# Down projection of both SwiGLU layers by chunk pairs, from seven Strassen block products

## The chip, the cores and the metric

The kernel runs on one core of one Trainium2 chip. The metric is device time in microseconds (us) of one execution. TensorE (PE) multiplies, with its weight loads shown as PEld; VectorE (DVE), ScalarE (ACT) and GpSimd (POOL) work elementwise; transfers are issued from the queues of SyncE (SP) and POOL and carried by 16 DMA engines.

## The reference

One decoder block over 256 tokens of width 2048, all in float32:

```python
x = LN(ALPHA*x + 0.5 * (silu(x@Wg1) * (x@Wu1)) @ Wd1)      # D_FF = 5632
x = LN(ALPHA*x + mixer(x))                                 # attention heads beside an RG-LRU, then w_out
x = LN(ALPHA*x + 0.5 * (silu(x@Wg2) * (x@Wu2)) @ Wd2)
x = x + sigmoid(x @ w_ple_gate) * (p @ w_ple_proj)
```

Weights come from HBM once each: `Wg`, `Wu` are 2048x5632 and `Wd` is 5632x2048. The change touches the product with `Wd1` and `Wd2`, (256x5632) @ (5632x2048).

## The kernel before

**Precision.** A float32 product is made of three fp32r products: each operand is split into `hi` (a rounding copy on ACT, L61 or L88) and `lo` (source minus hi on DVE, L62 or L94), and hi*hi, hi*lo and lo*hi are added up in one PSUM bank.

**Weights.** A list (`make_plan`) holds every weight tile of 256 rows x 512 columns ("entry", 512 KB) in the order in which PE uses them. SP loads an entry into a `raw` buffer (5 of them, L71); ACT makes `hi`, DVE makes `lo` (9 buffers each). `advance` prepares up to 7 entries beyond the one that PE holds, and loads are issued three entries beyond the one that is cast.

**SwiGLU** (`swiglu`, L405) goes over 11 chunks of 512 hidden units. A chunk takes 8 gate entries and 8 up entries (`group_a`: per entry 16 matmuls on hi, 512 columns, and on lo, 256 columns, into four banks), evacuated by ACT and DVE (L309, L310, L414, L415, L426) and split (L61, L62) into the activations of the chunk. Then come 8 down entries of the chunk before (`down`): for each of four column blocks of 512 and each of two token blocks of 128, 12 matmuls of 512 columns into a bank, which one DVE operation adds to the accumulator `acc` in SBUF (L315 the first time, L317 after). So a chunk's down projection takes 96 matmuls and 8 additions to `acc`. The last chunk's down (`down_last`) is joined with the LayerNorm that follows.

**Order.** Every engine works its queue in the order in which the program is written; nothing is reordered. A queue waits at its head: SP for a free `raw`, ACT for a loaded `raw` and a free `hi`, DVE for `hi` or for a finished bank. POOL does little: the LayerNorm residuals, a few `lo`, some small transfers.

Of the kernel before, what the change touches and what calls it, by code (L numbers as in the profile page):

```python
# [5 lines left out]
F32 = mybir.dt.float32  # L6
# [11 lines left out]
NCH = FF // 512  # L18
# [6 lines left out]
ALPHA = 2.0 ** 0.25  # L25
# [12 lines left out]
class Block:  # L38
# [105 lines left out]
    def make_plan(self):  # L144
        i = self.i
        plan = self.plan = []

        def add(w, r0, c0, n=1, **kw):
            for j in range(n):
                plan.append({"src": self.rows2(w, r0 + 256 * j, c0), "work": False, "pool": False,  # L150
                             "parts": [slice(0, 2)], "stationary": False, **kw})

        def ffn(name):
            g, u, d = (i[f"{name}_w_{v}"] for v in ("gate", "up", "down"))
            for c in range(NCH):
# [80 lines left out]
    def group_a(self, on_block, boundary=False):  # L236
        banks = [self.bank() for _ in range(4)]
        if not boundary:
            for j in range(8):
                e = self.take()  # L240
                self.tokens_a(e, j, banks, slice(0, 256), True, on_block)
                self.done(e)
                self.tick()
            return
# [85 lines left out]
    def down(self, acts, first):  # L330
        for n in range(4):
# [71 lines left out]

    def swiglu(self, boundary):
        nc = self.nc  # L405
        pend = None
        for c in range(NCH):
            gate = []

            def on_gate(b, bank):  # L410
# [7 lines left out]
            self.group_a(on_gate, boundary and c == 0)  # L418
            if c == 1 and not boundary:
                self.res_q.append(self.tables())  # L420
            ah, al = self.wide_r(), self.wide_r()

            def on_up(b, bank):
                u = self.narrow()
                self.evac_a(bank, u)
                nc.vector.scalar_tensor_tensor(u, gate[b], 0.5, u, op0=ALU.mult, op1=ALU.mult)  # L426
                self.split(ah[:, b, :], al[:, b, :], u)
# [217 lines left out]

    def mixer(self):
        nc = self.nc
        self.v = self.wide((P, 2, 512))
        self.group_b(lambda t, bank: nc.scalar.copy(self.v[:, t, :], bank), boundary=True)
        self.hs = []  # L650
# [66 lines left out]
        self.split(self.xT[:, 2 * j:2 * j + 2, 0, :], self.xT[:, 2 * j:2 * j + 2, 1, :], raw)  # L717

    def load_p(self):
        self.praw = self.narrow(), self.narrow()  # L720
        for k in range(2):
            self.nc.sync.dma_start(self.praw[k], self.i["pT"][k * P:(k + 1) * P, :])

    def split_p(self):
        self.pT, self.pp = self.wide_r(), []
        for k in range(2):
            self.split(self.pT[:, k, :], self.pT[:, 2 + k, :], self.praw[k])

    def load_acc(self, j):
        t, h = j % 2, j // 2  # L730
# [3 lines left out]
    def build(self):  # L734
        tc = self.tc
        with (
            tc.tile_pool(name="wraw", bufs=5) as self.wraw,
            tc.tile_pool(name="whi", bufs=SLOTS) as self.whi,
            tc.tile_pool(name="wlo", bufs=SLOTS) as self.wlo,
            tc.tile_pool(name="work", bufs=12) as self.work,  # L740
# [61 lines left out]
```

## Time and profile before

| | |
|---|---|
| time, median of 3 runs (lowest to highest) | 1930.77 us (1929.12 to 1932.76) |
| the profiled execution: its time, and its span | 1930.92 us, 1929.2 us |
| PE busy | 1916.6 us, 99% |
| weight loads (PEld) busy | 1654.4 us, 86% |
| DVE, ACT, POOL busy | 1290.9 us (67%), 961.8 us (50%), 151.1 us (8%) |
| bytes moved by DMA | 375.27 MB, 195 GB/s over the span |

The span is the profiled part of an execution; 1.7 us lie around it. Busy matmuls overlap in the profile (a matmul of 512 columns is shown as about 390 ns though the next starts after some 227 ns), so the pace of PE is read from starts. The first SwiGLU lies at about 5 to 720 us of the span, the second at about 1080 to 1815 us.

### The profile page before, as it was taken

The page shows a single profiled execution, that of the slowest core. Times are in us where ns is not written, and L with a number is a line of the kernel's source. Part 1 is how long each engine was busy: PE and PEld are TensorE (multiplying, and loading weights), DVE is VectorE, ACT ScalarE, POOL GpSimd, SP SyncE. Part 2 cuts the span into 40 slices and gives each one's busy share as a digit, 9 for nine tenths or more (in the row PEclk, how much of TensorE's full clock was granted, in tenths as well). Part 3 has the DMA queues.
Part 4 walks back from the last instruction along what each step waited for, and adds up shares of the span by engine and source line. Part 5 has one row for each costly group of instructions (what it writes and reads, how often), then busy time and mean ns, then how long its engine had stood idle before and what let it go on. Part 6 is the DMA issues. An engine that isn't in the chain of part 4 may idle for free.

```text
span 1929.2 us, 26578 instructions
## 1 busy us (share of the span) xinstructions
PE 1916.6 (99%) x10244; PEld 1654.4 (86%) x10244; DVE 1290.9 (67%) x1679; ACT 961.8 (50%) x1330; POOL 151.1 (8%) x93
## 2 busy tenths in 40 slices
PE   8999999999999999999999999999999999999999
PEld 7888888888888888888888898888888888888787
DVE  6667565756665666878777786566656756565875
ACT  6544444544444446656754545444444444454552
POOL 0000000000000012301100250000000000000151
PEclk9999999999999999999999999999999999999999
DMA  9666565556655666755465466656565556655564
GB/s 318 210 214 200 172 218 196 178 175 219 208 179 178 197 207 189 226 174 164 148 193 198 148 209 221 203 175 219 171 219 177 196 173 222 195 176 176 177 220 141
DMA packets 195007, 375.27 MB, mean 195 GB/s; under 512 B 11953, under 2 KB 14657, under 8 KB 194881
## 3 DMA queue, kind: packets, MB, share of 16 engines
q1 hardware_dynamic: 193856, 370.42, 58.6%
q0 software_dynamic: 1024, 3.16, 0.5%
q8 instruction: 80, 1.31, 0.3%
q14 instruction: 47, 0.38, 0.1%
HBM read 371.43 MB, written 2.10 MB: 194 GB/s over the span
## 4 chain that ended last, share of the span: by engine, by line
PE 99%; DVE 1%; DMA 0%; issue 0%; ACT 0%; SPq 0%; POOL 0%; DVEq 0%
PE mm L205 98%; PE mm L382 1%; DVE w L62 0%; DMA raw<-in_ffn_w_gate_dram 0%; DVE lo L94 0%; PE mm L588 0%; DVE bst L360 0%; DVE acc L317 0%; ACT hi L88 0%; POOL rs L369 0%; DVE acc L372 0%; SPq L71 0%; PE mm L620 0%; PE mm L619 0%; SPq L713 0%
## 5 line engine op out<-in xcount | busy, mean ns | idle before, releaser
L205 PE MATMUL mm<-xT,hi 128*128 128x512 f32 (+1 forms) x3216 | 1096.0, 390 | 6.1 <-DVE xT L62 5.0
L88 ACT CAST hi<-raw 128x1024 fp32r<-128x1024 f32 (+1 forms) x676 | 692.8, 1048 | 603.6 <-PE mm L205 399.4
L94 DVE TENSOR_TENSOR lo<-raw,hi 128x1024 fp32r<-128x1024 f32 (+1 forms) x676 | 837.6, 1277 | 219.0 <-ACT hi L88 218.3
L205 PE MATMUL mm<-xT,lo 128*128 128x256 f32 (+1 forms) x3216 | 887.6, 276 | 0.0
L205 PEld LDWEIGHTS mm<-xT,hi 128*128 128x128 f32 x3216 | 604.9, 188 | 130.7 <-ACT hi L88 6.3
L205 PEld LDWEIGHTS mm<-xT,lo 128*128 128x128 f32 x3216 | 606.2, 189 | 1.7 <-DVE lo L94 0.7
L205 PE MATMUL mm<-hi,w 128*128 128x512 f32 x1672 | 521.4, 390 | 0.0
L205 PEld LDWEIGHTS mm<-hi,w 128*128 128x128 f32 x1672 | 313.9, 188 | 65.4
L205 PE MATMUL mm<-lo,w 128*128 128x512 f32 x836 | 325.7, 390 | 0.6 <-DVE lo L94 0.6
L310 DVE TENSOR_TENSOR w<-mm,w 128x256 f32<-128x256 f32 x200 | 83.3, 419 | 184.3 <-ACT w L309 184.3
L205 PEld LDWEIGHTS mm<-lo,w 128*128 128x128 f32 x836 | 157.0, 188 | 32.5 <-DVE lo L94 1.0
L205 PE MATMUL mm<-hi,xT 128*128 128x512 f32 (+1 forms) x584 | 178.2, 382 | 0.0
L317 DVE TENSOR_TENSOR acc<-acc,mm 128x512 f32<-128x512 f32 x184 | 122.0, 680 | 62.3 <-PE mm L205 62.3
L94 POOL TENSOR_TENSOR w<-raw,w 128x1024 fp32r<-128x1024 f32 x9 | 26.0, 2912 | 1297.8 <-ACT w L88 669.2
L309 ACT COPY w<-mm 128x256 f32<-128x256 f32 x200 | 72.5, 366 | 107.7 <-PE mm L205 107.6
L205 PEld LDWEIGHTS mm<-hi,xT 128*128 128x128 f32 x584 | 107.7, 188 | 20.1
L205 PE MATMUL mm<-lo,xT 128*128 128x512 f32 (+1 forms) x292 | 110.4, 378 | 0.0
L61 ACT CAST w<-w 128x256 fp32r<-128x256 f32 x90 | 36.5, 406 | 92.0 <-DVE w L426 92.0
L62 DVE TENSOR_TENSOR w<-w,w 128x256 fp32r<-128x256 f32 x90 | 43.2, 480 | 41.8 <-ACT w L61 41.8
L415 DVE TENSOR_TENSOR w<-w,w 128x256 f32<-128x256 f32 x88 | 38.6, 439 | 44.3 <-ACT w L414 44.3
L205 PEld LDWEIGHTS mm<-lo,xT 128*128 128x128 f32 x292 | 55.0, 188 | 9.6
L414 ACT ACTIVATE w<-w 128x256 f32<-128x256 f32 x88 | 36.8, 418 | 48.1 <-DVE w L310 48.1
(125 smaller groups left out, 624.4 us busy)
## 6 DMA issues: line engine op xcount, KB each, us to landing
raw<-in_ffn_w_up_dram SPq DMA_DIRECT2D x176, 512.0 KB, 4.7
raw<-in_ffn_w_down_dram SPq DMA_DIRECT2D x176, 512.0 KB, 4.8
raw<-in_ffn_w_gate_dram SPq DMA_DIRECT2D x175, 512.0 KB, 4.6
raw<-in_w_in_dram SPq DMA_DIRECT2D x88, 512.0 KB, 4.5
raw<-in_w_out_dram SPq DMA_DIRECT2D x32, 512.0 KB, 4.7
raw<-in_w_ple_gate_dram SPq DMA_DIRECT2D x32, 512.0 KB, 5.0
w<-in_ln_g_dram SPq DMA_DIRECT2D x12, 256.0 KB, 8.7
w<-in_ln_b_dram SPq DMA_DIRECT2D x12, 256.0 KB, 8.0
```

What stands on the lines that cost most here:

```text
L61: self.nc.scalar.copy(hi, src)
L62: (self.nc.gpsimd if pool else self.nc.vector).tensor_tensor(lo, src, hi.bitcast(F32), op=ALU.subtract)
L88: self.nc.scalar.copy(e["hi"][:, k, :], e["raw"][:, k, :])
L94: eng.tensor_tensor(e["lo"][:, k, :], e["raw"][:, k, :], e["hi"][:, k, :].bitcast(F32), op=ALU.subtract)
L205: self.nc.tensor.matmul(out, lhsT=lhsT, rhs=rhs, start=start, stop=stop, skip_group_check=True)
L309: self.nc.scalar.copy(c, bank[:, 256:])
L310: self.nc.vector.tensor_tensor(dst, bank[:, :256], c, op=ALU.add)
L317: self.nc.vector.tensor_tensor(a, a, bank, op=ALU.add)
L382: nc.tensor.transpose(bank[:, q * P:(q + 1) * P], self.acc[:, t, kb * P:(kb + 1) * P], self.ident)
L414: nc.scalar.activation(s, g, AF.Sigmoid)
L415: nc.vector.tensor_tensor(g, g, s, op=ALU.mult)
```

## The change

Two neighbouring chunks of 512 hidden units and two column blocks of 512 of `Wd` form a 2x2 block product (the two token blocks x two chunks by two chunks x two column blocks), which is taken from seven block products (`p1` to `p7`, Winograd's form of Strassen) in place of eight. Each takes two entries and 12 matmuls of 512 columns. Chunks 0 to 9 make five pairs in each SwiGLU; chunk 10 stays with `down_last`.

- `make_forms` builds, after a pair's second up group, the seven left operands (four differences and sums, seven splits of 128 x 512).
- The right operands are single blocks of `Wd` or sums of two to four of them. The sums are made by transfers that add into `raw` (`accum_op=ALU.add`, issued from POOL): `p7` is loaded by SP and then added to (`plus`); `p5`, `p6` and `p4` are grown, each from the `raw` of the one before it in the chain `p1`, `p5`, `p6`, `p4`, once that has been cast (`grow`). Each is then cast to `hi` and `lo` as any entry.
- The 14 products of a pair (two halves of `Wd`'s columns) are run one at a time between the entries of the next two chunks: after each second gate or up entry, and in chunk 10 after each one.
- There are now 7 `raw` buffers (5 before), and 8 `hi` and 8 `lo` (9 before).

```diff
-SLOTS = 9
+SLOTS = 8
+RAWS = 7
+ORDER = ("p1", "p2", "p5", "p3", "p6", "p7", "p4")
...
+        if e.get("grows"):
+            return
         e["raw"] = self.tile(self.wraw, [P, 2, 512], F32, "raw")
         for k in e["parts"]:
             self.nc.sync.dma_start(e["raw"][:, k, :], e["src"][:, k, :])
+        if e.get("plus") is not None:
+            self.nc.gpsimd.dma_start(e["raw"], e["plus"], accum_op=ALU.add)
+
+    def grow(self, e):
+        n = e.get("next")
+        if n is not None:
+            n["raw"] = e["raw"]
+            self.nc.gpsimd.dma_start(n["raw"], n["src"], accum_op=ALU.add)
...
+        self.grow(e)
...
             for c in range(NCH):
-                add(g, 0, c * 512, 8, stationary=True)
-                add(u, 0, c * 512, 8, stationary=True)
-                if c:
-                    down(d, (c - 1) * 512)
+                step = 1 if c == NCH - 1 else 2
+                for w in (g, u):
+                    for j in range(8):
+                        add(w, 256 * j, c * 512, stationary=True)
+                        if j % step == step - 1 and todo:
+                            todo.pop(0)()
+                if c % 2:
+                    todo = blocks(d, (c - 1) * 512, 0) + blocks(d, (c - 1) * 512, 2)
...
+    def product(self):
...
+        kind, n = self.products.pop(0)
+        if kind in ("p1", "p2", "p5"):
+            self.pbank[kind] = self.bank()
+        bank = self.pbank[{"p2": "p2", "p5": "p5", "p3": "p5"}.get(kind, "p1")]
+        f = self.forms[kind]
+        es = []
+        for j in range(2):
+            e = self.take()
...
+            for k in range(2):
+                q = 2 * j + k
+                self.mm_moving_w(bank, (f[:, 0, q, :], f[:, 1, q, :]), e["hi"][:, k, :], e["lo"][:, k, :],
+                                 kind in ("p1", "p2", "p5") and q == 0, q == 3)
...
+            if (t, n + h) in self.untouched:
+                self.untouched.remove((t, n + h))
+                self.nc.vector.scalar_tensor_tensor(a, a, ALPHA, bank, op0=ALU.mult, op1=op)
+            else:
+                self.nc.vector.tensor_tensor(a, a, bank, op=op)
...
+    def make_forms(self, h0, h1):
...
+        put("p1", h0[:, :, a])
+        put("p2", h1[:, :, a])
+        nc.vector.tensor_tensor(s1, h1[:, :, b], h0[:, :, b], op=ALU.subtract)
+        put("p5", s1)
+        nc.vector.scalar_tensor_tensor(s2, s1, -1.0, h0[:, :, a], op0=ALU.mult, op1=ALU.subtract)
+        nc.vector.scalar_tensor_tensor(s4, s2, -1.0, h1[:, :, a], op0=ALU.mult, op1=ALU.subtract)
+        put("p3", s4)
+        put("p6", s2)
+        nc.vector.tensor_tensor(s3, h0[:, :, a], h0[:, :, b], op=ALU.subtract)
+        put("p7", s3)
+        put("p4", h1[:, :, b])
+        self.products = [(kind, n) for n in (0, 2) for kind in ORDER]
...
             self.group_a(on_gate, boundary and c == 0, step)
...
-            self.group_a(on_up)
-            if pend is not None:
-                self.down(pend, c == 1)
-            pend = (ah, al)
+            self.group_a(on_up, step=step)
+            if c % 2:
+                self.make_forms(before, h)
+            before = h
         self.down_last(pend)
```

Each product is added to `acc` once, and its split activations are no longer made per chunk but per pair. The queues show it at two places of the first SwiGLU.

DVE at the end of the up group of chunk 1, before (`mm` a PSUM bank, `w` a work buffer, L310 to L62 the evacuation and the split of the last block, L94 a `lo`, L315 an addition to `acc`):

```order
L310 TENSOR_TENSOR w_186_1054<-mm_813,w_187_1055 128x256
L426 SCALAR_TENSOR_TENSOR w_186_1054<-w_144_801,w_186_1054 128x256
L62 TENSOR_TENSOR w_148_809<-w_186_1054,w_147_808 128x256
L94 TENSOR_TENSOR lo_1014<-raw_945,hi_1013 128x1024
L94 TENSOR_TENSOR lo_1064<-raw_967,hi_1063 128x1024
L315 SCALAR_TENSOR_TENSOR acc<-acc,mm_1073 128x512
```

And now (L350 and L528 the same evacuation, L64 the splits of the seven left operands, L423 to L429 their sums and differences, L106 a `lo`):

```order
L350 TENSOR_TENSOR w_142_795<-mm_799,w_177_1033 128x256
L528 SCALAR_TENSOR_TENSOR w_142_795<-w_139_788,w_142_795 128x256
L64 TENSOR_TENSOR w_180_1039<-w_69_384,w_180_1039 128x512
L64 TENSOR_TENSOR w_181_1042<-w_142_795,w_181_1042 128x512
L423 TENSOR_TENSOR w_178_1037<-w_142_795,w_69_384 128x512
L64 TENSOR_TENSOR w_182_1046<-w_178_1037,w_182_1046 128x512
L425 SCALAR_TENSOR_TENSOR w_178_1037<-w_178_1037,w_69_384 128x512
L426 SCALAR_TENSOR_TENSOR w_179_1038<-w_178_1037,w_142_795 128x512
L64 TENSOR_TENSOR w_183_1051<-w_179_1038,w_183_1051 128x512
L64 TENSOR_TENSOR w_184_1054<-w_178_1037,w_184_1054 128x512
L429 TENSOR_TENSOR w_179_1038<-w_69_384 128x512
L64 TENSOR_TENSOR w_185_1058<-w_179_1038,w_185_1058 128x512
```

Eleven operations of 128 x 512 (the last one follows below) now stand between the last evacuation and the next `lo`, where before the next `lo` followed at once.

POOL after its first transfers in the first SwiGLU, before (L94 are three `lo` at the first LayerNorm, at 709 us):

```order
L461 DMA posi_905<-in_pos_dram 128x2
L465 DMA w_163_904<-in_inv_dram 128x16
L94 TENSOR_TENSOR w_1217_6434<-raw_6383,w_1216_6433 128x1024
L94 TENSOR_TENSOR w_1221_6455<-raw_6389,w_1220_6454 128x1024
```

And now (L83 is a transfer that grows the `raw` of a chain, L77 the one that adds to a `p7`; `raw_800` and `raw_825` are the two halves of the chain of the first pair's first product set):

```order
L568 DMA w_157_890<-in_inv_dram 128x16
L83 DMA raw_800<-in_ffn_w_down_dram 128x2x512
L83 DMA raw_825<-in_ffn_w_down_dram 128x2x512
L83 DMA raw_800<-in_ffn_w_down_dram 128x2x512
L83 DMA raw_825<-in_ffn_w_down_dram 128x2x512
L77 DMA raw_1272<-in_ffn_w_down_dram 128x2x512
L83 DMA raw_800<-in_ffn_w_down_dram 128x2x512
L77 DMA raw_1296<-in_ffn_w_down_dram 128x2x512
L83 DMA raw_825<-in_ffn_w_down_dram 128x2x512
```

POOL's queue, which was empty here until the first LayerNorm, now carries 8 adding transfers for each half pair, and the last growth of each chain stands behind a `p7` addition that waits for SP's load.

## Rows read from the trace of the kernel before

**Rows 1.** The page: busy time by engine, and the chain that ended last.

```profile
PE 1916.6 (99%) x10244; PEld 1654.4 (86%) x10244; DVE 1290.9 (67%) x1679; ACT 961.8 (50%) x1330; POOL 151.1 (8%) x93
...
PE 99%; DVE 1%; DMA 0%; issue 0%; ACT 0%; SPq 0%; POOL 0%; DVEq 0%
```

**Rows 2.** Windows of two chunks each; length, busy (x instructions), clock, DMA, GB/s.

```profile
core 0: us, PE busy (x) PEld busy (x) DVE busy (x) ACT busy (x) POOL busy (x), PEclk, DMA share, GB/s
316.52:446.80 130.28, 130.28 (x704) 112.76 (x703) 81.59 (x104) 59.82 (x80) 0.00 (x0) 1.00 0.59 193
446.80:577.00 130.20, 130.20 (x704) 112.69 (x703) 81.59 (x104) 59.68 (x81) 0.00 (x0) 1.00 0.59 193
```

**Rows 3.** Timeline of PE: a down projection's first matmul; start, busy.

```profile
294.74 0.40 PE L205 MATMUL mm<-hi,w 128*128 128x512 f32 x1
```

**Rows 4.** Timeline of PE: the next gate group's first matmuls.

```profile
316.52 0.40 PE L205 MATMUL mm<-xT,hi 128*128 128x512 f32 x1
...
316.76 0.28 PE L205 MATMUL mm<-xT,lo 128*128 128x256 f32 x1
...
316.88 0.39 PE L205 MATMUL mm<-xT,hi 128*128 128x512 f32 x1
...
317.10 0.28 PE L205 MATMUL mm<-xT,lo 128*128 128x256 f32 x1
```

**Rows 5.** Groups on DVE, 316.5 to 447 us; busy, mean ns, idle before.

```profile
L94 DVE TENSOR_TENSOR lo<-raw,hi 128x1024 fp32r<-128x1024 f32 x48 | 56.7, 1220 | 17.4 <-ACT hi L88 17.4
L317 DVE TENSOR_TENSOR acc<-acc,mm 128x512 f32<-128x512 f32 x16 | 10.6, 681 | 6.3 <-PE mm L205 6.3
L310 DVE TENSOR_TENSOR w<-mm,w 128x256 f32<-128x256 f32 x16 | 6.7, 419 | 17.4 <-ACT w L309 17.4
L415 DVE TENSOR_TENSOR w<-w,w 128x256 f32<-128x256 f32 x8 | 3.4, 426 | 3.9 <-ACT w L414 3.9
L62 DVE TENSOR_TENSOR w<-w,w 128x256 fp32r<-128x256 f32 x8 | 3.4, 426 | 3.8 <-ACT w L61 3.8
L426 DVE SCALAR_TENSOR_TENSOR w<-w,w 128x256 f32<-128x256 f32 x8 | 3.4, 426 | 0.3
```

**Rows 6.** Groups on ACT in the same stretch.

```profile
L88 ACT CAST hi<-raw 128x1024 fp32r<-128x1024 f32 x48 | 49.2, 1048 | 48.3 <-PE mm L205 38.2 <-DMA raw<-in_ffn_w_gate_dram 5.2 <-DMA raw<-in_ffn_w_down_dram 4.9
L309 ACT COPY w<-mm 128x256 f32<-128x256 f32 x16 | 5.8, 365 | 10.0 <-PE mm L205 10.0
L61 ACT CAST w<-w 128x256 fp32r<-128x256 f32 x8 | 3.3, 407 | 8.0 <-DVE w L426 8.0
```

**Rows 7.** Groups of the whole span: elementwise work of 128 x 512.

```profile
L61 ACT CAST xT<-qk 128x512 fp32r<-128x512 f32 x24 | 14.9, 621 | 0.8
...
L62 DVE TENSOR_TENSOR xT<-w,xT 128x512 fp32r<-128x512 f32 x8 | 5.5, 686 | 4.2 <-ACT xT L61 4.2
```

**Rows 8.** Windows in which the DMA engines are full, in the first chunk.

```profile
45.00:50.00 5.00, 5.00 (x30) 4.37 (x29) 2.45 (x2) 2.09 (x3) 0.00 (x0) 1.00 1.04 391
50.00:55.00 5.00, 5.00 (x30) 4.39 (x29) 2.48 (x5) 2.89 (x5) 0.00 (x0) 1.00 1.05 390
```

**Rows 9.** Transfers by line; KB each, median us from issue to landing.

```profile
raw<-in_ffn_w_down_dram SPq DMA_DIRECT2D x176, 512.0 KB, 4.8
...
w<-in_w_rgate_dram POOLq DMA_DIRECT2D x3, 256.0 KB, 3.3
```

**Rows 10.** Timeline of POOL: the issue of a transfer.

```profile
786.97 0.82 POOL L506 DMA_DIRECT2D w<-in_w_rgate_dram  x1
```

**Rows 11.** Waits of SP's queue: us in total, times, longest.

```profile
SPq L71 <- DVE lo L94: 1503.2, 634, 13.3
```

More of the change, by code (lines that the diff above doesn't have):

```diff
@@ L154, in ffn, with blocks, entries @@
             g, u, d = (i[f"{name}_w_{v}"] for v in ("gate", "up", "down"))
+            todo = []
             for c in range(NCH):
-                add(g, 0, c * 512, 8, stationary=True)
-                add(u, 0, c * 512, 8, stationary=True)
-                if c:
-                    down(d, (c - 1) * 512)
-            down(d, (NCH - 1) * 512)
+                step = 1 if c == NCH - 1 else 2
[6 more added lines that the diff above has]
+                    todo = blocks(d, (c - 1) * 512, 0) + blocks(d, (c - 1) * 512, 2)
+            down(d, (NCH - 1) * 512)
+        def blocks(w, r0, n):
+            chain = [None, None]
+            def entries(kind):
+                for j in range(2):
+                    r, c = r0 + 256 * j, n * 512
+                    at = {"p1": (0, 0), "p2": (512, 0), "p5": (0, 512), "p3": (512, 512),
+                          "p6": (512, 512), "p7": (0, 512), "p4": (512, 0)}[kind]
+                    add(w, r + at[0], c + at[1], kind=kind)
+                    e = plan[-1]
+                    if kind == "p7":
+                        e["plus"] = self.rows2(w, r + 512, c + 512)
+                    if kind in ("p5", "p6", "p4"):
+                        e["grows"] = True
+                        chain[j]["next"] = e
+                    if kind in ("p1", "p5", "p6"):
+                        chain[j] = e
+            return [lambda kind=kind: entries(kind) for kind in ORDER]
         def down(w, r0):
@@ L234, in tokens_b, with group_a @@
             self.mm_moving_w(bank[:, cols], self.x_act(kb, t), e["hi"][:, k, cols], e["lo"][:, k, cols], kb == 0, kb == KB - 1)
[L236 removed]
+    def group_a(self, on_block, boundary=False, step=2):
         banks = [self.bank() for _ in range(4)]
@@ L243, in group_a @@
                 self.tick()
+                if j % step == step - 1:
+                    self.product()
             return
@@ L337, in down @@
                 self.done(e)
+    def product(self):
+        if not self.products:
+            return
+        kind, n = self.products.pop(0)
[4 more added lines that the diff above has]
+        es = []
+        for j in range(2):
+            e = self.take()
+            assert e["kind"] == kind
+            es.append(e)
+            for k in range(2):
+                q = 2 * j + k
+                self.mm_moving_w(bank, (f[:, 0, q, :], f[:, 1, q, :]), e["hi"][:, k, :], e["lo"][:, k, :],
+                                 kind in ("p1", "p2", "p5") and q == 0, q == 3)
+        for t, h, op in {"p1": [(0, 0, ALU.add)], "p2": [(0, 0, ALU.add)], "p5": [(1, 1, ALU.subtract)],
+                         "p3": [(0, 1, ALU.subtract)], "p6": [(0, 1, ALU.subtract)],
+                         "p7": [(1, 1, ALU.subtract)], "p4": [(1, 0, ALU.add)]}[kind]:
+            a = self.acc[:, t, (n + h) * 512:(n + h + 1) * 512]
+            if (t, n + h) in self.untouched:
[3 more added lines that the diff above has]
+                self.nc.vector.tensor_tensor(a, a, bank, op=op)
+        for e in es:
+            self.done(e)
@@ new lines, in make_forms, with put @@
+    def make_forms(self, h0, h1):
+        nc = self.nc
+        a, b = slice(0, P), slice(P, 256)
+        z = self.wide((P, 2, 4, P)), self.wide((P, 2, 4, P))
+        s1, s2, s3, s4 = z[0][:, 0], z[0][:, 1], z[1][:, 0], z[1][:, 1]
+        self.forms = {}
+        def put(kind, src):
+            f = self.forms[kind] = self.wide_r((P, 2, 4, P))
+            self.split(f[:, 0], f[:, 1], src)
+        put("p1", h0[:, :, a])
[10 more added lines that the diff above has]
+        self.products = [(kind, n) for n in (0, 2) for kind in ORDER]
@@ L405, in swiglu @@
         nc = self.nc
-        pend = None
+        self.products, self.pbank = [], {}
+        self.untouched = {(t, n) for t in range(2) for n in range(4)}
+        before = None
         for c in range(NCH):
             gate = []
+            last = c == NCH - 1
+            step = 1 if last else 2
             def on_gate(b, bank):
@@ L416, in on_gate @@
                 gate.append(g)
-            self.group_a(on_gate, boundary and c == 0)
+            self.group_a(on_gate, boundary and c == 0, step)
             if c == 1 and not boundary:
                 self.res_q.append(self.tables())
-            ah, al = self.wide_r(), self.wide_r()
+            if last:
+                pend = self.wide_r(), self.wide_r()
+            else:
+                h = self.wide()
             def on_up(b, bank):
-                u = self.narrow()
+                u = self.narrow() if last else h[:, b, :]
                 self.evac_a(bank, u)
                 nc.vector.scalar_tensor_tensor(u, gate[b], 0.5, u, op0=ALU.mult, op1=ALU.mult)
-                self.split(ah[:, b, :], al[:, b, :], u)
-            self.group_a(on_up)
-            if pend is not None:
-                self.down(pend, c == 1)
-            pend = (ah, al)
+                if last:
+                    self.split(pend[0][:, b, :], pend[1][:, b, :], u)
+            self.group_a(on_up, step=step)
+            if c % 2:
+                self.make_forms(before, h)
+            before = h
         self.down_last(pend)
@@ L647, in mixer @@
         nc = self.nc
+        self.products = []
         self.v = self.wide((P, 2, 512))
@@ L719, in load_p @@
     def load_p(self):
-        self.praw = self.narrow(), self.narrow()
+        self.praw = self.tile(self.qk, [P, 2, 256], F32, "qk")
         for k in range(2):
-            self.nc.sync.dma_start(self.praw[k], self.i["pT"][k * P:(k + 1) * P, :])
+            self.nc.sync.dma_start(self.praw[:, k, :], self.i["pT"][k * P:(k + 1) * P, :])
     def split_p(self):
@@ L726, in split_p @@
         for k in range(2):
-            self.split(self.pT[:, k, :], self.pT[:, 2 + k, :], self.praw[k])
+            self.split(self.pT[:, k, :], self.pT[:, 2 + k, :], self.praw[:, k, :])
     def load_acc(self, j):
@@ L736, in build @@
         with (
-            tc.tile_pool(name="wraw", bufs=5) as self.wraw,
+            tc.tile_pool(name="wraw", bufs=RAWS) as self.wraw,
             tc.tile_pool(name="whi", bufs=SLOTS) as self.whi,
```

## The prediction

> **What bounds the kernel now.** I read the page's busy times and its chain first: PE is busy for 99% of the span and the chain is PE for 99% [rows 1]. Then the windows, to see whether that holds in the stage that is changed: two successive stretches of two chunks take 130.28 and 130.20 us, PE is busy for all of either, with 704 matmuls, at a granted clock of 1.00, while DVE works 81.6 us, ACT 59.8 us and the DMA engines 0.59 of the time [rows 2]. So a matmul less is time less, until another engine takes more than what is left. The groups of DVE and ACT [rows 5, 6], the full DMA windows [rows 8] and SP's waits [rows 11] tell how near each is to that. SP waits 1503 us for DVE's `lo` to free a `raw`: transfers start when a buffer comes free, not when a DMA engine does.
>
> **What it removes.** A down projection runs from its first matmul at 294.74 us [rows 3] to the next gate group's at 316.52 us [rows 4]: 96 matmuls in 21.78 us, 0.2269 us each. A pair of chunks falls from 2 x 96 = 192 to 14 products x 12 = 168. Five pairs in each of two SwiGLUs: 2 x 5 x 24 = 240 matmuls, 240 x 0.2269 = **54.45 us** on PE, which is the path. A gate or up entry stays as it is: (130.28 - 2 x 21.78) / 32 = 2.71 us. So a pair's stretch should take 130.28 - 24 x 0.2269 = 124.8 us of PE, and chunk 10, which carries all 14 products of the fifth pair beside its 16 entries, 16 x 2.71 + 168 x 0.2269 = 81.5 us. These two are what every other engine has to stay below.
>
> **What it adds, engine by engine.**
> ACT: 12 more casts of about 1.03 us (49.2 / 48) [rows 6] and seven copies of 0.62 [rows 7] for eight of 0.41 [rows 6]: 59.8 + 12.3 + 4.3 - 3.3 = 73 of 124.8 us. Hidden by PE.
> DVE: 60 `lo` for 48, at 56.7 / 48 = 1.18 us: 70.8. 14 additions to `acc` for 16, at 0.66: 9.3. Evacuation 6.7 + 3.4 + 3.4 = 13.5 [rows 5]. Eleven operations of 128 x 512 for the left operands, at 0.69 [rows 7]: 7.6. With the waits for ACT inside this work (3.9 at L415 [rows 5], three of 0.62 where a copy follows a sum) it is 107 of 124.8 us: still below PE. In chunk 10 it is 44 x 1.18 + 14 x 0.66 + 8.4 (evacuation and its own split) + 7.6 + 5.8 (waits) = 83 against PE's 81.5: level.
> POOL: 16 issues a pair at 0.82 us [rows 10], 13 us. Hidden.
> DMA: an entry alone, at the 390 GB/s of the full windows [rows 8], is 524,288 B / 390 = 1.34 us of all engines. A pair's stretch has 32 gate and up loads, 16 plain loads for products and 16 adding ones: 48 x 1.34 + 16 p = 64.3 + 16 p, with p the price of an adding transfer.
>
> **The unknown price.** The trace has no adding transfer. The least is that of a plain one, 1.34 us (the same bytes come out of HBM). At the most its three moves, a read of the source, a read of the target and the write, take a plain transfer's time each: 4.02 us. No row lies nearer to one end, and I take the middle, two plain transfers, p = 2.68. Then a pair's stretch has 107.2 us of DMA under 124.8 of PE, and chunk 10 has 32 x 1.34 + 16 x 2.68 = 85.8 over 81.5: 4.3 us a SwiGLU, **8.6 us** in all. At p = 1.34 it is 85.7 and 64.3 us, at no cost; at 4.02, 128.6 and 107.2 us, over PE in both places.
> The Trainium skill ("Collectives: The Full Stack", section "The bandwidth ceiling: the fold count and why AG ≠ RS ≠ AR") says that a reducing transfer is halved by its two source reads on one ring and not by the add itself; by it p would be two plain transfers and the sum the one given here. No run here shows it yet.
> The full windows move 390 and 391 GB/s. The Trainium skill ("DMA: Bandwidth & Descriptors", section "Specifications") puts what one core can draw from HBM at about 358 GB/s, which the rows contradict for ten microseconds on end; if it held over a long stretch, an entry would be 1.46 us, chunk 10 would have 93.7 us of DMA, and the time would be 16 us above my figure.
>
> **Where covers are thin.** Between the last evacuation of a pair and the next `lo`, DVE now has the left operands. Ahead of that stand six prepared entries. In a plain stretch these are four gate entries and `p1`: 4 x 2.71 + 2.72 = 13.6 us of PE. DVE needs a tail of 0.37 + 0.42 + 0.43 us [rows 5, 6], 7.6 + 1.9 us for the operands and 1.18 for the `lo`: 11.9 us. Covered, with 1.7 to spare; if it isn't, about 2 us at each of eight places, 16. In chunk 10 the six entries are two gate entries and two products, 10.9 us: 1.0 us short, **2 us** for both SwiGLUs.
> A switch between the two kinds of matmul costs a little: the first start after it is 0.24 us off, then 0.22 [rows 4]. 200 to 250 more switches: **3 us**, between 0 and 6.
> The chain: a growth is issued when the `lo` of the block before it is done, and the next block of the chain is eight entries on (six in chunk 10), 124.8 / 60 x 8 = 16.6 us or 81.5 / 44 x 6 = 11.1 us. Issue 0.82, and a landing between 4.8 us (a plain entry [rows 9]) and three times that, taken as twice, 9.6: 10.4 us. In time in both places. On POOL the addition to a `p7` waits for SP's load, and behind it stands the growth of `p6` into `p4`, which ACT's cast waits for: up to 4.8 us later, 15.2 us, still in time in a plain stretch and 4.1 us late in chunk 10. A `p7` holds its `raw` for SP's load, 4.8, the issue, the addition and the casts, 4.8 + 0.8 + 9.6 + 2.2 = 17.4 us, while a buffer of the five that the chain leaves free comes round in seven entries, 14.6 or 13.0 us. It is 3 to 4 us late, and ACT's queue stands behind it, and DVE's, and SP's for the buffers; but PE has six entries in hand (11 to 12.5 us), and DVE refills them at 1.18 against 2.08 us. Nothing on PE.
> One `hi` and `lo` slot less outside the SwiGLUs: I cost it at nothing, since the two extra `raw` stand in for it and PE is the chain there as well [rows 1].
>
> **Sum.** Profiled execution 1930.92 (the median of the runs, 1930.77, is the same) - 54.45 + 8.6 + 2 + 3 = **1890 us**.
>
> **Rivals.**
> *Adding transfers are cheap and all covers hold.* Only the matmuls go: 1930.92 - 54.45 = 1876.5, some 1880 with the switches. For it: PE's 99%. Against: no transfer that reads two operands has been seen at a plain one's price.
> *Adding transfers are late, not too many.* They share the engines with SP's loads, and the two `p7` and six chain links of chunk 10 have no spare DVE time to catch up in. With a landing in 12 us a link is late by 0.8 + 12 - 11.1 = 1.7 us, a `p7` by 4.8 + 0.8 + 12 + 2.2 - 13.0 = 6.8: 6 x 1.7 + 2 x 6.8 = 24 us, less the 11.1 in hand, 13 a SwiGLU: 26 more, 1916. For it: loads wait for buffers already [rows 11]. Against: the adding transfers have a queue of their own.
> *The DMA engines become the bound, and it is slower.* At p = 4.02 the plain stretches exceed PE by 3.8 us, eight times, and chunk 10 by 25.7, twice: 82 in place of 8.6, 1930.92 - 54.45 + 82 + 5 = 1963. Its point is p = 3.8: there 8 x 0.3 + 2 x 22.2 + 5 make up for most of the 54, and each further 0.1 costs 16 us. For it: 14 products now need 28 entries and 32 transfers where 16 did. Against: 0.59 of the engines' time is all that the stretch uses today [rows 2].
> *It does not remove what it says.* Excluded: 168 matmuls stand in PE's queue for each pair where 192 stood.
>
> **Chances.** A measurement tells 0.2%, some 4 us, from no change. My forecast (1882 to 1905) 0.50; cheap and covered (under 1882) 0.12; late (1905 to 1927) 0.16; DMA-bound 0.22, of which 0.04 within 0.2% and 0.18 slower. Faster 0.78, same 0.04, slower 0.18. The range reaches from just above 1876.5, the removed matmuls alone, to 1942 on the DMA-bound side, and leaves out some 0.15, nearly all above. The likeliest case by itself: 1882 to 1905.
>
> **What would show it.** Right: 240 matmuls fewer; the stretches of chunks 2 and 3 to 8 and 9 near 125 us with PE busy throughout; chunk 10 near 86 to 88, with ACT's `hi` waiting there for `raw` that are being added to; DVE above 80% and DMA near 0.85 in the stretch. Wrong: adding packets that take three times a plain one's time; PE waiting for `hi` or `lo` in every stretch; PE waiting at `p2` behind the left operands; or a granted clock below 1.00 where PE has begun to wait.

## The result and the profile after

The changed kernel takes 2053.94 us (median of 4 runs, 2045.61 to 2059.59), the kernel before, on the same chip, 1929.94 us (1928.15 to 1932.76). The ratio is 1.0638, with a 95% interval of 1.0598 to 1.0677: 6.4% slower, where 1890 us and at most 1942 were forecast.

The page of the changed kernel: busy time by engine, the two DMA queues (q1 carries SP's loads, q0 those that POOL issues; packets, MB, share of 16 engines' span), the chain, and the median landing of the transfers of `Wd`.

```profile
PE 1926.0 (94%) x10004; PEld 1643.0 (80%) x10004; DVE 1447.1 (70%) x1809; ACT 1088.4 (53%) x1440; POOL 344.8 (17%) x253
...
q1 hardware_dynamic: 193856, 370.42, 53.6%
q0 software_dynamic: 44544, 87.05, 24.6%
...
PE 51%; DMA 21%; DVE 11%; issue 10%; ACT 4%; POOL 1%; POOLq 0%; SPq 0%; DVEq 0%; ACTq 0%
...
raw<-in_ffn_w_down_dram SPq DMA_DIRECT2D x176, 512.0 KB, 6.2
...
raw<-in_ffn_w_down_dram POOLq DMA_DIRECT2D x160, 512.0 KB, 10.2
```

PE has its 240 matmuls less than in [rows 1], and yet is busy 9.4 us more; the chain, PE for 99% before, is PE for 51% and DMA for 21%. No engine is full: DVE has 70%. This is the picture of a kernel in which everybody waits a little for somebody, so the stage itself has to be read. Windows of two successive two-chunk stretches, from one first gate matmul to the next, and of the first 100 us of chunk 10 (columns as in [rows 2]):

```profile
238.72:378.19 139.47, 131.35 (x683) 112.22 (x682) 96.99 (x118) 72.86 (x91) 19.41 (x16) 0.96 0.88 241
378.19:518.32 140.13, 132.43 (x683) 113.02 (x681) 96.98 (x118) 72.62 (x91) 19.39 (x16) 0.95 0.87 240
658.29:758.00 99.71, 77.96 (x375) 65.03 (x374) 64.51 (x76) 46.36 (x56) 16.84 (x14) 0.91 0.88 226
```

A stretch takes 139.5 to 140.1 us in place of the 124.8 forecast, and of the 130.3 of [rows 2]. (Those windows were cut short: the next gate groups begin at 447.16 and 577.80 us, so a stretch before takes 130.64 us, and the work with products is 130.64 - 24 x 0.2269 = 125.2 us.) PE stands for 8 us of it, and the granted clock is 0.95 to 0.96. DVE is busy 97.0 and ACT 72.9 us, no more than the forecast gave them. The DMA engines have a share of 0.88, so over the stretch they are not full either: something is late.

**Where the late thing is.** The waits of the changed kernel (engine, line, what it waited for; us in total, times, longest), then PE's own:

```profile
DVE lo L106 <- ACT hi L100: 297.3, 125, 8.4
ACT hi L100 <- DMA raw<-in_ffn_w_down_dram: 239.6, 78, 8.6
...
POOL raw L77 <- DMA raw<-in_ffn_w_down_dram: 106.6, 9, 14.6
```

```profile
PE mm L243 <- DVE acc L406: 79.9, 18, 9.2
PE mm L243 <- DVE w L350: 30.1, 13, 4.7
...
PE mm L243 <- DVE lo L106: 2.2, 2, 1.1
PE mm L243 <- ACT hi L100: 1.3, 1, 1.3
```

DVE waits for `hi`, and ACT for `Wd` blocks. PE itself waits for a weight (`hi` or `lo`) for only 3.5 us. For 110 us it waits for DVE: for the addition of a finished product to `acc` (L406), or for the evacuation of a finished gate bank (L350).

PE's last long stall in the stretch from 99.49 to 238.72 us, in the chain of waits (start, us, what):

```profile
184.49 6.82 DMA raw<-in_ffn_w_down_dram
...
191.99 0.62 POOL raw L77
...
193.39 14.14 DMA raw<-in_ffn_w_down_dram
...
207.63 1.05 ACT hi L100
...
208.71 1.22 DVE lo L106
209.93 0.43 DVE w L350
```

This is `p7`, which has two entries. SP can only start the first one's load at 184.49, when a `raw` comes free, and the second one's at 185.63. The first lands after 6.82 us, and its addition (L77, at 191.96) after 7.6: it is cast at 199.70, as early as the forecast had it. The second lands after 7.0 us, but its addition, issued at 193.39, takes 14.14 us; only then can ACT cast it, at 207.63. From its load to the end of its `lo`, at 209.93, it holds its `raw` for 24.3 us, and ACT and DVE, which work in order, stand behind it. In all 20 pairs of such additions the first takes 5.7 to 7.6 us and the second 9.2 to 14.8. The timeline of POOL shows why (start, length, what it issues; the length of an issue on POOL is rough):

```profile
191.96 1.19 POOL L77 DMA_DIRECT2D raw<-in_ffn_w_down_dram  x1 [14.00 <-DVE lo L106]
192.67 1.71 POOL L83 DMA_DIRECT2D raw<-in_ffn_w_down_dram  x1
193.39 2.21 POOL L77 DMA_DIRECT2D raw<-in_ffn_w_down_dram  x1
194.09 2.73 POOL L83 DMA_DIRECT2D raw<-in_ffn_w_down_dram  x1
```

Both additions of `p7` (L77) and both growths of `p6` into `p4` (L83) are issued within 2.1 us and share the engines (a DMA share of 1.10 at 203 to 207 us, below). A like burst stands at 133.76 to 135.89 us in the other column half, and PE's other long stall of the stretch follows it and ends at 151.22 us.

**How it reaches PE.** The timelines of ACT, DVE and PE at the end of the two stalls (in brackets the idle time before, and what ended it):

```profile
147.03 1.99 ACT L100 CAST hi<-raw 128x1024 fp32r<-128x1024 f32 x2 [6.06 <-DMA raw<-in_ffn_w_down_dram]
...
148.12 2.36 DVE L106 TENSOR_TENSOR lo<-raw,hi 128x1024 fp32r<-128x1024 f32 x2 [5.12 <-ACT hi L100]
150.39 0.68 DVE L406 TENSOR_TENSOR acc<-acc,mm 128x512 f32<-128x512 f32 x1
...
151.22 0.77 PE L243 MATMUL mm<-hi,w 128*128 128x512 f32 x1 [3.56 <-DVE acc L406]
```

```profile
207.63 1.99 ACT L100 CAST hi<-raw 128x1024 fp32r<-128x1024 f32 x2 [6.88 <-DMA raw<-in_ffn_w_down_dram]
209.53 0.36 ACT L349 COPY w<-mm 128x256 f32<-128x256 f32 x1
...
210.40 0.80 PE L243 MATMUL mm<-xT,hi 128*128 128x512 f32 x1 [3.41 <-DVE w L350]
```

In the first, PE has reached `p7`, whose first entry has been ready for over 4 us. But `p7` is added up in the bank of `p6`, and that bank must first be added to `acc` (L406). By the program's order this addition stands in DVE's queue behind the `lo` of the entries that are prepared ahead, the late second `p7` among them. In the second, an up group needs a bank of the gate group before it, whose evacuation (L349 on ACT, L350 on DVE) stands behind the cast of the late `p7`. Every one of the eight stretches has one long stall of either kind, of 2.4 to 7.5 us.

**What a stall costs.** Short windows around PE's stall, which ends at 210.40 us:

```profile
203.00:207.00 4.00, 3.99 (x21) 3.16 (x19) 0.00 (x0) 0.00 (x0) 0.00 (x0) 1.00 1.10 262
207.00:210.40 3.40, 0.00 (x0) 0.00 (x0) 1.64 (x2) 2.28 (x4) 0.00 (x0) 0.81 1.01 241
210.40:214.00 3.60, 3.60 (x11) 3.12 (x12) 2.21 (x6) 2.01 (x6) 0.00 (x0) 0.50 0.54 151
214.00:217.00 3.00, 2.89 (x11) 2.25 (x11) 2.52 (x5) 2.89 (x4) 0.00 (x0) 0.68 0.00 0
217.00:222.00 5.00, 5.00 (x26) 4.22 (x26) 5.00 (x6) 4.16 (x5) 0.00 (x0) 1.00 0.78 243
```

PE stands for 3.41 us, and then runs at a granted clock of 0.50, the lower of its two levels (1.2 GHz), until some 5 us after it began again: 11 matmuls in 3.60 us, where 21 took 4.00 before. So this stall costs its own length and some 2.6 us more. Over the whole run, against the kernel e4 below, which has the same 10004 matmuls at a clock of 1.00 and is busy 1870.5 of 1894.4 us, the changed kernel is longer by 163.1 us, of which 1926.0 - 1870.5 = 55.5 are matmuls at the lower clock and 107.6 are PE standing.

### The profile page after: what moved, and what is told of

Same layout as the page of the kernel before. It is cut to its first block, busy times and chain, and to the rows that moved or that the text cites. A ratio compares the mean times of both kernels' runs of the same rounds, so it can differ in the third digit from the quotient of the medians.

```text
span 2057.5 us, 27049 instructions
## 1 busy us (share of the span) xinstructions
PE 1926.0 (94%) x10004; PEld 1643.0 (80%) x10004; DVE 1447.1 (70%) x1809; ACT 1088.4 (53%) x1440; POOL 344.8 (17%) x253
## 3 DMA queue, kind: packets, MB, share of 16 engines
q1 hardware_dynamic: 193856, 370.42, 53.6%
q0 software_dynamic: 44544, 87.05, 24.6%
## 4 chain that ended last, share of the span: by engine, by line
PE 51%; DMA 21%; DVE 11%; issue 10%; ACT 4%; POOL 1%; POOLq 0%; SPq 0%; DVEq 0%; ACTq 0%
PE mm L243 50%; DMA raw<-in_ffn_w_down_dram 17%; DVE lo L106 4%; DMA raw<-in_ffn_w_up_dram 4%; ACT hi L100 2%; DVE w L64 2%; DVE w L350 1%; ACT w L63 1%; DVE acc L406 1%; DVE w L528 1%; ACT w L513 1%; POOL w L106 1%; DVE w L514 1%; PE mm L477 1%; POOL raw L77 1%
## 5 line engine op out<-in xcount | busy, mean ns | idle before, releaser
L100 ACT CAST hi<-raw 128x1024 fp32r<-128x1024 f32 (+1 forms) x796 | 810.2, 1047 | 730.5 <-PE mm L243 372.1
L106 DVE TENSOR_TENSOR lo<-raw,hi 128x1024 fp32r<-128x1024 f32 (+1 forms) x796 | 972.9, 1268 | 298.4 <-ACT hi L100 297.3
L243 PE MATMUL mm<-xT,hi 128*128 128x512 f32 (+1 forms) x3216 | 1127.9, 396 | 36.6 <-DVE w L350 30.1
L243 PE MATMUL mm<-xT,lo 128*128 128x256 f32 (+1 forms) x3216 | 897.4, 279 | 2.2 <-DVE lo L106 2.2
L243 PEld LDWEIGHTS mm<-hi,w 128*128 128x128 f32 x1512 | 294.8, 195 | 159.2 <-issue 45.9
L83 POOL DMA_DIRECT2D raw<-in_ffn_w_down_dram x120 | 173.7, 1530 | 900.2 <-DVE lo L106 841.2
L243 PE MATMUL mm<-lo,w 128*128 128x512 f32 x756 | 305.2, 404 | 0.0
L406 DVE TENSOR_TENSOR acc<-acc,mm 128x512 f32<-128x512 f32 x124 | 84.7, 683 | 98.6 <-PE mm L243 98.6
L350 DVE TENSOR_TENSOR w<-mm,w 128x256 f32<-128x256 f32 x200 | 83.0, 419 | 34.5 <-ACT w L349 34.1
L77 POOL DMA_DIRECT2D raw<-in_ffn_w_down_dram x40 | 62.2, 1555 | 260.4 <-DMA raw<-in_ffn_w_down_dram 106.6
L349 ACT COPY w<-mm 128x256 f32<-128x256 f32 x200 | 72.4, 364 | 19.8 <-PE mm L243 19.3
L63 ACT CAST w<-w 128x512 fp32r<-128x512 f32 (+1 forms) x78 | 44.7, 598 | 66.0 <-DVE w L426 20.9
L64 DVE TENSOR_TENSOR w<-w,w 128x512 fp32r<-128x512 f32 (+1 forms) x78 | 50.0, 662 | 25.3 <-ACT w L63 24.4
## 6 DMA issues: line engine op xcount, KB each, us to landing
raw<-in_ffn_w_down_dram POOLq DMA_DIRECT2D x160, 512.0 KB, 10.2
```

What stands on the lines that cost most here:

```text
L63: self.nc.scalar.copy(hi, src)
L64: (self.nc.gpsimd if pool else self.nc.vector).tensor_tensor(lo, src, hi.bitcast(F32), op=ALU.subtract)
L77: self.nc.gpsimd.dma_start(e["raw"], e["plus"], accum_op=ALU.add)
L83: self.nc.gpsimd.dma_start(n["raw"], n["src"], accum_op=ALU.add)
L100: self.nc.scalar.copy(e["hi"][:, k, :], e["raw"][:, k, :])
L243: self.nc.tensor.matmul(out, lhsT=lhsT, rhs=rhs, start=start, stop=stop, skip_group_check=True)
```

## The experiments

Twelve runs of ten kernels. One time each and one profile, if nothing else is said; the kernel before, beside them, took 1927.9 to 1931.2 us. The table shows the first SwiGLU from the starts of gate groups on PE: the mean of its four two-chunk stretches (work of 125.2 us with products) and the stretch from chunk 10's start to a fixed matmul in the mixer behind it. There the work is 158.0 - 21.78 + 168 x 0.2269 = 174.3 us with 14 products (the kernel before without its down projection of chunk 9), and about 180 in e5 and f3, 177 in f4. For f2 and f4 these two columns come from the slowest of their repeated runs (1943.43 and 1913.13 us); the traces of their single runs have 127.0 and 197.9, 126.8 and 180.4.

| kernel | what differs from the changed kernel | time, us | stretch | chunk 10 on |
|---|---|---|---|---|
| before | | 1929.94 | 130.6 | 158.0 |
| changed | | 2053.94 | 139.7 | 206.6 |
| e1 | no transfer adds | 1919.87 | 125.9 | 194.5 |
| e3 | `p7` alone isn't added to | 1914.99 | 126.2 | 190.5 |
| f1 | growth issued ahead of `p7`'s addition | 2099.07 | 143.2 | 211.2 |
| f2 | `p7` grown from `p3`'s `raw` | 1938.03 (median of 9) | 127.8 | 199.3 |
| e4 | f2, no transfer adds | 1896.54 | 125.7 | 182.9 |
| e5 | fifth pair by plain products | 2003.74 | 139.1 | 181.2 |
| f3 | f2 and e5 | 1912.09 | 127.3 | 181.2 |
| f4 | f2, fifth pair half by products | 1908.75 (median of 4) | 127.5 | 182.6 |
| g1 | as changed, fewer bytes | 2040.08 | 139.1 | 203.0 |
| g2 | f2, more bytes | 1945.87 | 128.3 | 203.4 |

**e1: what is the addition worth?**

```diff
-            self.nc.gpsimd.dma_start(e["raw"], e["plus"], accum_op=ALU.add)
+            self.nc.gpsimd.dma_start(e["raw"], e["plus"])
...
-            self.nc.gpsimd.dma_start(n["raw"], n["src"], accum_op=ALU.add)
+            self.nc.gpsimd.dma_start(n["raw"], n["src"])
```

> All 160 POOL transfers keep their place, size and waits but write instead of adding; the sums of weight blocks are left out, so five of the seven products use single blocks. Theory A (price): an adding transfer takes 3.1 us of all DMA engines by the packets of the changed kernel, a plain one 1.46, and a pair's stretch has about 120 us of DMA that comes in bursts; without the adding 94 us are left: 1880 to 1900 us, PE idle under 15 us, clock 1.00. Theory B (order): the burst comes from POOL's order, and p7 still waits for SP's load and holds up the last growth: 1890 to 1950 us. Theory C (casts): DVE and ACT, with 28 entries in place of 16 and the left operands, are late, whatever the transfers do: 2030 to 2060 us.

1919.87 us, in the range of B and 20 us above that of A. The stretches fall to 125.9 us although every cast, left operand and switch is there, and `p7` still takes two steps. So casts, DVE and the interleaving aren't the cause of what the stretches lose, and neither are two steps by themselves; the adding is a necessary part of it. Its q0 row gives the price beside the one above:

```profile
q0 software_dynamic: 24064, 87.05, 13.7%
```

The kernel before has 0.5% on q0. So an adding transfer takes (24.6 - 0.5)% x 2057.5 / 160 = 3.10 us of all 16 engines, a plain one (13.7 - 0.5)% x 1917.7 / 160 = 1.58, and one of SP's in the changed kernel, by its q1 row, 53.6% x 2057.5 / 370.42 MB x 0.524 MB = 1.56. The same bytes take 128 packets more for each adding transfer ((44544 - 24064) / 160), 272 against 144. The Trainium skill ("Collectives: The Full Stack", section "The bandwidth ceiling: the fold count and why AG ≠ RS ≠ AR") has a reducing transfer halved by its two source reads; a ratio of 1.96 to 1.99 agrees. That the reads are the reason is not shown here.

**e3: only `p7`'s addition away.**

```diff
-                    if kind == "p7":
-                        e["plus"] = self.rows2(w, r + 512, c + 512)
```

> Only the addition to p7 is left out (p7 multiplies a single block); the 120 growths stay. Theory A: 12 adding transfers a pair in place of 16, 107 us of DMA in a stretch of 125, and the burst of four adding transfers within 3 us at p7 becomes one of two: about half of the loss goes, 1950 to 1990 us. Theory B: nothing on POOL waits for an SP load any more, and the stalls at p4 and p7 go: 1890 to 1930 us. Theory C: 2040 to 2060 us.

1914.99 us, stretches of 126.2: with 120 of the 160 adding transfers still there, nearly all of the loss in the stretches is gone, as B expected. It leaves out 4 x 3.1 us of DMA work a pair too, so it doesn't tell yet whether it is the order or the amount.

**f1: is it the growth that POOL holds up behind `p7`?** The forecast named this wait. Here the growth goes first.

```diff
-            self.nc.gpsimd.dma_start(e["raw"], e["plus"], accum_op=ALU.add)
+            self.late.append(e)
...
+            if self.late:
+                m = self.late.pop(0)
+                self.nc.gpsimd.dma_start(m["raw"], m["plus"], accum_op=ALU.add)
```

> The same work; on POOL the growth of p6 into p4 is issued ahead of the addition to p7, which stood before it. Theory A: the same transfers meet on the same engines, 2030 to 2060 us. Theory B: the last growth is no longer held up by up to 5 us; the stalls before p4 go and those before p7 stay: 1980 to 2020 us. Theory C: 2040 to 2060 us.

2099.07 us, which none of the theories had: 45 us slower than the changed kernel. POOL's four issues still lie within 2.2 us, with `p7`'s two now each behind a growth, and the stretches grow by 3.5 us. The growth of `p4` wasn't the late item in the stretches. Its trace shows why 0.7 us of issue costs 3.5: the second addition to `p7` is issued that much later and takes 1.1 to 1.2 us longer besides (13.0 and 15.2 us in the first stretch, for 11.8 and 14.1), and a stretch has two of them; its two long stalls are 5.50 and 5.09 us, for 3.56 and 3.41.

**f2: the same sum without the two steps.** `p7` needs `p3`'s block and one more, so it can grow in `p3`'s `raw`, as the chain does: no load by SP, one addition.

```diff
-            chain = [None, None]
+            chain, side = [None, None], [None, None]
...
                     if kind == "p7":
-                        e["plus"] = self.rows2(w, r + 512, c + 512)
+                        e["grows"] = True
+                        side[j]["next"] = e
+                    if kind == "p3":
+                        side[j] = e
```

> The same result; the weights of p7 are grown from the raw of p3 (one of its two blocks is p3's) when p3 is cast, in place of an SP load with an addition behind it: 8 plain transfers a pair fewer out of 48, and the addition is issued some eight entries earlier. Adding transfers stay 16 a pair. Theory A: 108 us of DMA in a stretch of 125 and about 85 in chunk 10, still bursts: 1940 to 1990 us. Theory B: no addition waits for a load, none stands ahead of the last growth, no burst: 1895 to 1930 us. Theory C: 2040 to 2060 us.

The sum in this text has a slip: it is four plain transfers a pair less, not eight, so 44 x 1.46 + 16 x 3.10 = 113.8 us (118 with the 1.56 of the row above; no row shows 1.46). Its single run gave 1937.74 us, between the two ranges. Timed again:

> The same kernel as f2_p7_from_p3 (p7 grown from p3's raw buffer, five pairs by products), now timed several times. Its single run gave 1937.74 us beside 1927.88 to 1930.77 of the kernel before. If the loss left in chunk 10 (about 24 us over its work) eats all that the 240 products save, it comes to 1933 to 1942 us, 0.2 to 0.6 per cent slower than before; if the single run lay high by chance, 1925 to 1932, no difference.

1938.03 us (median of 9 runs, 1933.01 to 1943.43), 1.0041 of before, interval 1.0027 to 1.0054: 116 us of the loss gone, and with all 160 adding transfers left. POOL's timeline of f2 shows the additions apart:

```profile
169.71 2.42 POOL L83 DMA_DIRECT2D raw<-in_ffn_w_down_dram  x2 [14.10 <-DVE lo L106]
177.80 2.42 POOL L83 DMA_DIRECT2D raw<-in_ffn_w_down_dram  x2 [5.67 <-DMA raw<-in_ffn_w_gate_dram]
186.00 2.42 POOL L83 DMA_DIRECT2D raw<-in_ffn_w_down_dram  x2 [5.79 <-DVE lo L106]
```

Two at a time, some 8 us apart, where the changed kernel issued four at once. The median landing of all 160 is no shorter (10.4 us). f2 takes three things away together: the load ahead of the addition, the `raw` that this load claims, and the burst. Which of them weighs how much was not tried; more `raw` buffers, or an earlier load of `p7`, would tell.

**g1 and g2: order or amount?** With the measured prices the changed kernel has 48 x 1.56 + 16 x 3.10 = 124.5 us of DMA work in a stretch of 125.2 us of PE, f2 118. A rival could say that only the 6.2 us matter. g1 gives the changed kernel f2's amount, g2 gives f2 the changed kernel's.

```diff
+                        if c > 1 and j % (4 if c < NCH - 1 else 2) == 1:
+                            plan[-1]["short"] = True
...
+        if e.get("short"):
+            self.nc.sync.dma_start(e["raw"][:, 0:1, :], e["src"][:, 0:1, :])
+            e["raw"] = e["raw"][:, 0:1, :].to_broadcast([P, 2, 512])
+            return
```

> The changed kernel, its p7 still fetched in two steps, but from chunk 2 on every fourth gate and up entry (every second in chunk 10) loads only its first 128 rows and uses them twice, so half of that weight block is left out. A pair then has 8 half loads, 8 x 0.78 = 6.2 us less for the DMA engines: 118 us instead of 48 x 1.56 + 16 x 3.10 = 124.5, the same as the kernel whose p7 grows out of p3. A: p7 is late because its two steps come one behind the other; the stretches stay at 136 to 140 us and the time at 2010 to 2045. B: the order does not matter, the DMA engines merely have 124.5 us of work under 124.8 us of PE; with 118 the stretches fall to 126 to 129 us and the time to 1930 to 1955.

```diff
+                        if c > 1 and (j == 5 or c == NCH - 1 and j == 2):
+                            plan[-1]["again"] = True
...
+        if e.get("again"):
+            for k in range(2):
+                self.nc.sync.dma_start(self.tile(self.qk, [P, 512], F32, "qk"), e["src"][:, k, :])
```

> The kernel whose p7 grows out of p3 (f2), with 4 gate and up entries a pair loaded a second time, by SP, into buffers that nobody reads: 4 x 1.56 = 6.2 us more for the DMA engines a pair, 124.5 us, the same as the changed kernel has. A: only p7's two steps cost; the stretches stay at 126 to 129 us, chunk 10 loses a little more, 1938 to 1965 us. B: 124.5 us of DMA work under 124.8 us of PE is what costs; the stretches go to 137 to 141 us and the time to 2020 to 2055.

g1 took 2040.08 us, g2 1945.87: both as A had it. Two stretches of g1:

```profile
238.99:379.05 140.06, 130.57 (x682) 111.78 (x681) 97.13 (x118) 72.78 (x91) 19.42 (x16) 0.96 0.85 225
379.05:516.66 137.61, 130.53 (x682) 111.91 (x681) 97.11 (x118) 72.76 (x91) 19.39 (x16) 0.96 0.86 230
```

Two of g2:

```profile
355.01:482.34 127.33, 126.35 (x682) 108.86 (x681) 96.88 (x118) 72.95 (x91) 19.29 (x16) 1.00 0.95 264
482.34:608.50 126.16, 126.07 (x682) 108.77 (x681) 96.77 (x118) 73.22 (x91) 19.29 (x16) 1.00 0.95 269
```

The DMA engines can be busy for 0.95 of a stretch, and PE stands for 1.0 or 0.1 us of it; and they can be at 0.85, and it stands for 7 to 9.5. How `p7` is fetched decides; the amount moves a stretch by 0.5 to 1.2 us. (In chunk 10, where g2 is 4 to 5.5 us longer than f2, the amount does count.)

**e5, e4, f3: the rest, in chunk 10.** f2 still has 25 us over its work there.

```diff
-                step = 1 if c == NCH - 1 else 2
+                step = 2
...
+                    if c == NCH - 2:
+                        todo = todo[:7 * HALVES]
+            for n in range(2 * HALVES, 4):
+                for q in (NCH - 3, NCH - 2):
+                    add(d, q * 512, n * 512, 2)
```

With `HALVES = 0` this runs the fifth pair after chunk 10, by plain products.

> The changed kernel with its two-step p7, but the fifth pair of each SwiGLU is projected by plain blocks after chunk 10, and chunk 10 carries no products. Theory B as it now stands (a p7 that takes an SP load and then an addition in a burst is late in every stretch): the four stretches of two chunks stay near 140 us each; with chunk 10 as before the change it is 94.4 + 4 x 139.7 + 21.8 = 675 us up to chunk 10 against 638 before, twice 37 more: about 2004 us. If chunk 10 were the cause of most of it: 1930 to 1960.

2003.74 us, as B had it: the stretches stay at 139.1, the chunk 10 part takes 181.2 us for 180 of work. So the products in chunk 10 account for 50 us of the time, net of the 48 matmuls that they save, and the four pairs for the rest of the loss.

> f2_p7_from_p3 with the 160 POOL transfers writing in place of adding; the sums of weight blocks are left out. What is left of f2's 1938 us: if the price of adding still decides in chunk 10 (0.90 of the DMA engines' time there), the stretch from chunk 10 to the transposes falls from 198 to about 178 us and the time to 1890 to 1900. If it is DVE, whose work of 83 us there I put level with PE's 81.5, chunk 10 stays 12 us or more late: 1910 to 1925.

e4 is f2 with e1's edit. 1896.54 us: it lies in the range for the price of adding, and chunk 10's part falls from 199.3 to 182.9, not quite to 178. A window of f2 in chunk 10, then one of e4:

```profile
607.26:702.00 94.74, 80.00 (x388) 66.63 (x387) 66.63 (x78) 47.64 (x57) 16.71 (x14) 0.95 0.88 220
```

```profile
600.56:690.00 89.44, 85.40 (x435) 71.46 (x433) 74.89 (x92) 53.42 (x67) 9.94 (x14) 1.00 0.77 265
```

DVE, which the forecast had level with PE here, is busy for 75 of 89 us when the adding is free and PE nearly full. It is not the bound.

> f2 (p7 grown from p3) with the fifth pair of each SwiGLU by plain blocks after chunk 10. Same result. Stretches of 127 us in place of 130.6, and chunk 10 as before the change: 94.1 + 4 x 127 + 21.8 = 624 against 638 us up to chunk 10, twice 14 less than 1929: about 1901 us, 1895 to 1908. If the loss of f2 were spread over all stretches, 1920 or more.

f3 (f2's and e5's edits together) took 1912.09 us, 4 us above its range. Its stretches are 127.3, where 127 was taken, which is 2 us of it; the rest was not followed.

**f4: what the runs point to.** `HALVES = 1` with f2's edit: one column half of the fifth pair by products, after every second entry of chunk 10, the other by plain ones.

> As f3, but the first half of the fifth pair's columns is done by seven products in chunk 10, one after each second entry as in the stretches before it, and only the other half by plain blocks. 12 matmuls fewer a SwiGLU than f3, 2.7 us, with about 57 us of DMA in 62 of PE there: 1896 us, 1890 to 1904; if chunk 10 has no room for products at any pace, above f3.

1904.49 us in its single run. Timed again:

> The same kernel as f4_four_pairs_half (f2 with the fifth pair half by products, one product after every two entries in chunk 10), timed several times. Its single run gave 1904.49 us. If the cause is the late p7 and the price of the adding transfers in chunk 10, it stays at 1902 to 1908 us, 1.1 to 1.4 per cent faster than before and 7 per cent faster than the changed kernel; if that single run was luck, 1910 to 1925.

1908.75 us (median of 4 runs, 1904.06 to 1913.13), 0.9884 of before, interval 0.9863 to 0.9904; a little above the range given for it. It beats the kernel before by 1.2% and the changed one by 7%. It saves 216 matmuls, 49 us by [rows 3, 4]; about 21 are kept.

## Why the prediction was wrong

**What held.** The 240 matmuls are gone (10244 to 10004), and a stretch without late transfers takes 125.7 to 125.9 us (e4, e1), 0.5 to 0.7 above the 125.2 of work; that is the most that the switches can cost a stretch, 4 to 6 us in the eight, where 3 (0 to 6) were forecast. The forecast's own 124.8 came from windows cut 0.4 us short. ACT's 73 us is 72.9. For DVE 101 us of work (107 with waits) were forecast, 97.0 are busy. The left operands, thinnest of the covers, cost a stretch nothing that shows; in chunk 10 PE waits for the `lo` behind them for 1.1 us, twice, where 2 us in all were forecast. POOL is busy 19.4 us, not 13, still hidden.

**Sizes that were off, and small.** The price of an adding transfer was taken as 2.68 us; it is 3.10, inside its bounds. By the forecast's own formula chunk 10 then has 32 x 1.34 + 16 x 3.10 = 92.5 us of DMA over 81.5, 22 us for both SwiGLUs in place of 8.6: 1903 us. With a plain entry at 1.56, by the same measure as the 3.10, it has 99.5, 36 us: 1917. Neither gives 2054. The DMA-bound rival needed 3.8 and didn't come about.

**The step that failed** is this one: "A `p7` holds its `raw` for SP's load, 4.8, the issue, the addition and the casts, 4.8 + 0.8 + 9.6 + 2.2 = 17.4 us", "It is 3 to 4 us late", "but PE has six entries in hand (11 to 12.5 us), and DVE refills them at 1.18 against 2.08 us. Nothing on PE." Two things were wrong in it.

The hold: the first entry of the `p7` above took 17.5 us, as forecast, but the second 7.0 for the load, 0.8 to the addition's issue, 14.1 for the addition and 2.4 for the casts, 24.3 us. Against the 14.6 of a round of buffers that is 9.7 us late, some three times the figure. I had taken the plain landing of [rows 9], 4.8 us, and doubled it; here four that add are issued at once, together with SP's loads.

The cover: six entries in hand cover a PE that waits for weights, and PE hardly ever did (3.5 us in the run). It waited, for 110 us, for banks: for DVE's addition of a product (before `p7`, that of `p6`) and for the evacuation of a gate bank, which stand behind the late entry in DVE's and ACT's queues. The depth of the stock works against itself there, for an addition is queued behind the `lo` of what was prepared ahead of it. I had no term for this. It is read from the traces; no run puts the additions ahead of the `lo`.

f2 takes the load out of `p7`'s path and 116 us go; g1 and g2 show that it is the way in which `p7` is fetched and not the amount.

**What follows from it.** The excess over the removed matmuls, 1930.92 - 54.45 = 1876.5, is 4 x (139.7 - 125.2) + 4 x (140.4 - 125.2) = 119 us in the stretches (the second SwiGLU's take 140.4 us on average) and 2 x (206.6 - 174.3) = 65 in chunk 10, if the second is like the first: 2060, against the 2059.59 us of the profiled execution. The rival "adding transfers are late" was nearest to the mechanism; I gave it 1916, because it charged chunk 10 alone, deducted the stock in full there, and had PE's clock unchanged. That the clock could fall where PE waits stood in my list of what would prove me wrong, without a price in any case; it is 55 us.

**Still open.** In chunk 10 both parts are needed to get near its work: without the price of adding but with `p7`'s two steps it takes 194.5 us (e1), with the price and one step 199.3 (f2), without either 182.9 (e4). The traces show where PE stands: at `p7` again, waiting for the addition of `p6`. With a product after every entry, the `lo` of the first `p4` entry stands ahead of that addition as well, and this entry's growth takes 13.4 us in the changed kernel (stalls of 9.2 and 9.1 us in the first SwiGLU), 12.3 and 13.7 in f2 (3.8 and 5.5), 8.6 and 9.8 in e1 (3.8 and 4.4). No run tries that link by itself.

## What to carry to other kernels

When a transfer is put behind another transfer, count from the moment at which its buffer is claimed to the moment at which it is given back, with landings as they are when several are under way at once; a queue that works in order turns one late item into a wait of everything behind it. A stock of prepared work covers a late item only if nothing else that the bottleneck needs stands behind that item in the same queue: here the additions and evacuations that give PE its banks back stood behind the casts of entries that PE did not need yet. Where a sum can be made by adding to a buffer that is there already, that takes one step off the path at no cost in bytes.

## What the hardware showed unexpectedly

- After a stall of PE of 3.4 us the granted clock was 0.50, and some 5 us of matmuls went by before it was 1.00 again; PE is busy 55.5 us longer in the run than with the same matmuls at 1.00 (e4).
- A transfer that adds takes 3.10 us of the 16 engines for 512 KB, where a plain one of the same queue takes 1.58, and lands after 10.2 us (median) instead of 6.6 (e1's).
- Of two additions issued 1.4 us apart among four, the first landed after 7.6 us and the second after 14.1.
- The DMA engines held a share of 0.95 for whole stretches (g2) while PE stood for 1.0 us or less of either.
